# Issuing what follows a score group behind the group's last maximum on VectorE, in a decoder layer on one core

## The chip, the cores and the metric

The kernel runs on one core of one Trainium2 chip. The metric is the device time of one execution in microseconds (us). Three executions of the kernel before took 313.03, 313.59 and 314.9 us; their median, 313.59 us, is the time before. A further execution was profiled; it took 314.14 us.

## What is computed

One decoder layer on 256 tokens of width 1024, all in float32. Both head groups take q, k and v from one projection, their outputs are mixed by one output projection, a gated feed-forward layer follows, and each half ends in a layer norm:

```python
def reference(x, w_in, diff_lambda, diff_subln_g, w_o, ln1_g, ln1_b, w_ffn_in, w_ffn_out, ln2_g, ln2_b):
    ...
        proj = jnp.einsum('bsd,de->bse', x, w_in[l])
        dq, dk, dv, mq, mk, mv = jnp.split(proj, splits, axis=-1)
        a_out = diff_attention(dq, dk, dv, diff_lambda[l], diff_subln_g[l], lambda_init, cos, sin)
        b_out = moba_attention(mq, mk, mv, cos, sin)
        mix = jnp.einsum('bse,ed->bsd', jnp.concatenate([a_out, b_out], axis=-1), w_o[l])
        x = layer_norm(ALPHA * x + mix, ln1_g[l], ln1_b[l])
        gu = jnp.einsum('bsd,df->bsf', x, w_ffn_in[l])
        g, u = jnp.split(gu, 2, axis=-1)
        f = jnp.einsum('bsf,fd->bsd', jax.nn.silu(g) * u, w_ffn_out[l])
        x = layer_norm(ALPHA * x + f, ln2_g[l], ln2_b[l])
```

Differential attention takes the softmax of pairs of heads and subtracts one, times a factor, from the other. With 256 tokens the block-sparse attention is plain causal attention over one block. So both head groups compute eight causal softmaxes over scores of 256 queries by 256 keys.

## The kernel before

Every float32 product is split in two parts, `hi` (rounded) and `lo` (the rest), and summed from three matmuls (`mm3`, lines 150 to 153). Weights arrive in units of 1 MB (`raw`, four buffers); ScalarE casts a quarter of a unit at a time to `hi` (line 106) and VectorE subtracts to get `lo` (line 107). A buffer of `raw` comes free, and its next load is issued by SyncE, when the split of the unit before in it is done.

The input projection runs as `proj_qkT(0)` to `proj_qkT(3)` (q and k of the first group, then of the second) and `proj_v(4)`, `proj_v(5)`. Call c uses the units 2c and 2c+1. Each is a loop of 32 (or 16) steps n of three matmuls each, and other work is hung onto the steps of it by dictionaries, `side` (attention and rope) and `bg` (splits of the units to come), run at line 410. Scores of the first group are taken in two halves, `scores(0, 0)` and `scores(0, 1)`, at the steps 15 and 28 of `proj_qkT(2)`; those of the second group at the steps 5 and 11 of `proj_v(4)`.

One call of `scores(g, b)` (line 280) takes four PSUM buffers of the pool `psB`, which has four in all, fills them by 48 short matmuls (line 290), and then for each of the four sub-heads takes, on VectorE, the masked row maximum of a 128x128 and of a 128x256 piece (line 295; eight in all, each with a short read of its accumulator, and listed as CUSTOM_DVE in the trace and as ISA in the listing of the order), and on ScalarE the exponential of each (line 298). A buffer is free again when VectorE has taken both maxima of it. So the next group of scores needs the maxima of the group before.

`rope(c, bs, ps)` (line 244) has three VectorE operations that read the projection's PSUM (a shuffle into `sh`, line 253, and two products into `a` and `sh`, lines 254 and 255) and a `finish` (lines 258 to 260: an addition into `a`, a cast on ScalarE to `h`, and the subtraction to `l`). `plain` (line 264) is a cast and a subtraction (lines 269 and 270). `diff_combine` (line 312) runs at step 12 of `proj_qkT(3)`: a reciprocal `rl`, two small operations into `sc` (lines 315 to 317) and eight combinations on VectorE (line 320), two per head. From step 22 on `diff_pt(h)` transposes head h of the result on TensorE (lines 303 to 305).

Each engine runs its instructions in one order, fixed when the program is built. This order is not the order in which the code is written: a scheduler places every instruction on its engine at the time at which it expects it to be ready. `tc.issue_after(ins)` adds edges to it: what the block issues on the engine of `ins` is ordered behind `ins`, with no semaphore.

Of the kernel before, what the change touches and what calls it, by code (L numbers as in the profile page):

```python
# [37 lines left out]
FIN0, FIN1, FIN2, FIN3 = (20, 26), (4, 7), 31, 20  # L38
# [18 lines left out]
def hybrid_layer_kernel(ctx, tc, xT, xr, w_in, w_o, w_f1, w_f2, cols, rows, lamb, rot, tri, out):  # L57
    nc = tc.nc
# [65 lines left out]
    def spread(units_, pieces, steps):  # L124

        gens = [(u, p) for u in units_ for p in range(pieces)]
        live = {}

        def emit(u):
            if u not in live:  # L130
                live[u] = split_gen(u, pieces)
                state["split"] = u + 1
            next(live[u])

        hooks = {}
        for i, (u, p) in enumerate(gens):
            hooks.setdefault(i * steps // len(gens), []).append(lambda u=u: emit(u))
        return hooks

    def ahead(u, loads=4, splits=2):  # L140
        while state["load"] <= min(u + loads, NU - 1):
            n = state["load"]
            load_unit(n, LOAD_PIECES.get(n, 1))
            state["load"] += 1
        while state["split"] <= min(u + splits, NU - 1):
            n = state["split"]
            split_unit(n, SPLIT_PIECES.get(n, 2))
            state["split"] += 1

    def mm3(ps, sh, sl, mh, ml, first, last):  # L150
        nc.tensor.matmul(ps, sh, mh, start=first, stop=False)  # L151
        nc.tensor.matmul(ps, sh, ml, start=False, stop=False)  # L152
        nc.tensor.matmul(ps, sl, mh, start=False, stop=last)  # L153
# [81 lines left out]
    def qk_tiles(c, part):  # L235
        QH[c, part] = apool.tile([P, 2, S], F32R, tag=f"h{c % 2}{part}", name=f"h{c}_{part}")
        QL[c, part] = apool.tile([P, 2, S], F32R, tag=f"l{c % 2}{part}", name=f"l{c}_{part}")
# [7 lines left out]
    def rope(c, bs, ps):  # L245

        m = bs.stop - bs.start
        if bs.start == 0:
            qk_tiles(c, 0)
            SH[c] = rpool.tile([P, 2, S], F32, tag="sh", name=f"sh{c}", bufs=2)  # L250
            QA[c] = rpool.tile([P, 2, S], F32, tag="qk", name=f"a{c}", bufs=2)
        sh, a, h, l = SH[c][:, bs, :], QA[c][:, bs, :], QH[c, 0][:, bs, :], QL[c, 0][:, bs, :]
        nc.vector.stream_shuffle(sh, ps, SWAP)
        nc.vector.tensor_mul(a, ps, cos2[:, :m, :])
        nc.vector.tensor_mul(sh, sh, sin2[:, :m, :])

        def finish():
            nc.vector.tensor_add(a, a, sh)
            nc.scalar.copy(h, a)
            nc.vector.tensor_sub(l, a, h.bitcast(F32))  # L260

        return finish

    def plain(c, bs, ps):

        if bs.start == 0:
            qk_tiles(c, 1)
        h, l = QH[c, 1][:, bs, :], QL[c, 1][:, bs, :]
        nc.scalar.copy(h, ps)
        nc.vector.tensor_sub(l, ps, h.bitcast(F32))  # L270

    E0, E1, negm, ls, rl = {}, {}, {}, {}, {}

    def alloc_group(g):
        E0[g] = epool.tile([P, 8, P], F32, tag=f"E0", name=f"E0{g}", bufs=1)
        E1[g] = epool.tile([P, 8, S], F32, tag=f"E1", name=f"E1{g}", bufs=1)
        negm[g] = small.tile([P, 2, 8], F32, tag="negm", name=f"negm{g}")
        ls[g] = small.tile([P, 2, 8], F32, tag="ls", name=f"ls{g}")
        rl[g] = small.tile([P, 2, 8], F32, tag="rl", name=f"rl{g}")

    def scores(g, b):

        cq, ck = 2 * g, 2 * g + 1
        pr = [psB.tile([P, 3 * P], F32, tag="b", name=f"s{g}_{b}_{s}") for s in range(4)]
        terms = [(A, B, part) for A, B in ((QH, QH), (QL, QH), (QH, QL)) for part in range(2)]
        for q, o, n in ((slice(P, S), 0, S), (slice(0, P), S, P)):
            for m, (A, B, part) in enumerate(terms):
                for s in range(4):
                    r = slice(32 * s, 32 * s + 32)
                    nc.tensor.matmul(pr[s][:, o : o + n], A[cq, part][r, b, q], B[ck, part][r, b, :n],  # L290
                                     start=m == 0, stop=m == len(terms) - 1)
        for s in range(4):
            u = 4 * b + s
            for i, (e, p, m) in enumerate(((E0[g][:, u, :], pr[s][:, S:], mask[:, P:]), (E1[g][:, u, :], pr[s][:, :S], mask))):
                nc.vector.tensor_tensor_reduce(  # L295
                    out=e, in0=p, in1=m, scale=-0.125, scalar=3.4e38, op0=ALU.add, op1=ALU.min,
                    accum_out=negm[g][:, i, u : u + 1])
                nc.scalar.activation(e, e, AF.Exp, bias=negm[g][:, i, u : u + 1], scale=-1.0,  # L298
                                     accum_out=ls[g][:, i, u : u + 1])

# [92 lines left out]
    def proj_tok(ps, c, t, k):  # L393
        u, i = 2 * c + k // 4, k % 4
        ts_ = slice(t * P, (t + 1) * P)
        mm3(ps, xTh[:, k, ts_], xTl[:, k, ts_], hi[u][:, i, :], lo[u][:, i, :], k == 0, k == KT - 1)

    def proj_qkT(c, side):

        pool, tag = (psB, "b") if c == 1 else (psA, "acc")  # L400
        pss = [pool.tile([P, 2, S], F32, tag=tag, name=f"pj{c}_{b}") for b in range(4 if c < 2 else 2)]
        kb = {0: 1, 1: 4}.get(c, KT)
        order = [(j, k0 + k) for k0 in range(0, KT, kb) for j in range(4) for k in range(kb)]
        fin = []
        ahead(2 * c, splits=-1)
        bg = spread([1] + [2] if c == 0 else [3, 4, 5] if c == 1 else [2 * c + 2, 2 * c + 3], 4, 28)
        for n, (j, k) in enumerate(order):
            if n == 16:
                ahead(2 * c + 1, splits=-1)
            for f in side.get(n, []) + bg.get(n, []):  # L410
                f()
            u, i = 2 * c + k // 4, k % 4
            ws = slice(j * P, (j + 1) * P)
            ps = pss[j][:, 0, :] if c < 2 else pss[j // 2][:, j % 2, :]
            mm3(ps, hi[u][:, i, ws], lo[u][:, i, ws], xTh[:, k, :], xTl[:, k, :], k == 0, k == KT - 1)
            if k == KT - 1 and c < 2:
                done = [j] if c else list(range(4)) if j == 3 else []
                for jj in done:
                    bs, p1 = slice(jj % 2, jj % 2 + 1), pss[jj][:, 0:1, :]
                    if jj < 2:  # L420
                        fin.append(rope(c, bs, p1))
                    else:
                        plain(c, bs, p1)
            elif k == KT - 1 and j == 1:
                side.setdefault((FIN2, FIN3)[c - 2], []).append(rope(c, slice(0, 2), pss[0]))
            elif k == KT - 1 and j == 3:
                plain(c, slice(0, 2), pss[1])
        return fin

    def proj_v(c, side):  # L430

        pss = [psA.tile([P, 512], F32, tag="acc", name=f"pj{c}_{t}") for t in range(2)]
        ahead(2 * c, splits=-1)
        bg = spread([2 * c + 2, 2 * c + 3], 4, 14)
        for n, (t, k) in enumerate((t, k) for t in range(2) for k in range(KT)):
            if n == 8:
                ahead(2 * c + 1, splits=-1)
            for f in side.get(n, []) + bg.get(n, []):
                f()
            proj_tok(pss[t], c, t, k)  # L440
            if k == KT - 1:
                nc.scalar.copy(V[c - 4][:, t, :], pss[t])

    fin = proj_qkT(0, {})
    nlam, gsub = lambda_prep()
    fin = proj_qkT(1, {FIN0[i]: [f] for i, f in enumerate(fin)})
    nc.sync.dma_start(x_sb, xr.rearrange("(t p) d -> p t d", p=P))
    alloc_group(0)
    sc = {FIN1[i]: [f] for i, f in enumerate(fin)}
    for b in range(2):  # L450
        sc.setdefault(SCORES0[b], []).append(lambda b=b: scores(0, b))
    proj_qkT(2, sc)
    sc = {COMBINE: [diff_combine]}
    for h in range(4):
        sc.setdefault(DIFF_PT[h], []).append(lambda h=h: diff_pt(h))
    proj_qkT(3, sc)
    alloc_group(1)
    proj_v(4, {SCORES1[b]: [lambda b=b: scores(1, b)] for b in range(2)})
    od = {}

# [8 lines left out]
    for n, u in enumerate(range(6)):  # L469
        sd.setdefault(8 + n, []).append(lambda u=u: moba_pt(u))  # L470
    proj_v(5, sd)


# [376 lines left out]
```

## Time and profile before

| what | before |
|---|---|
| median of three executions | 313.59 us (313.03 to 314.9) |
| the profiled execution | 314.14 us |
| its span, first to last instruction | 312.4 us |
| TensorE busy | 300.0 us, 96% of the span |
| VectorE busy | 242.4 us, 78% |
| ScalarE busy | 178.8 us, 57% |
| TensorE's share of the chain that ended last | 88% |

Times within a profile count from the start of its span. An instruction's duration in a row holds some tail that overlaps with the next row, so what one costs in a row of its kind is read from the start of one to the start of the next. TensorE's matmuls are pipelined in the same way. The granted clock is told as a share of full speed: 1.00 is 2.4 GHz and 0.50 is 1.2 GHz.

### The profile page before, as it was taken

The page shows a single profiled execution, that of the slowest core. Times are in us where ns is not written, and L with a number is a line of the kernel's source. Part 1 is how long each engine was busy: PE and PEld are TensorE (multiplying, and loading weights), DVE is VectorE, ACT ScalarE, POOL GpSimd, SP SyncE. Part 2 cuts the span into 40 slices and gives each one's busy share as a digit, 9 for nine tenths or more (in the row PEclk, how much of TensorE's full clock was granted, in tenths as well). Part 3 has the DMA queues.
Part 4 walks back from the last instruction along what each step waited for, and adds up shares of the span by engine and source line. Part 5 has one row for each costly group of instructions (what it writes and reads, how often), then busy time and mean ns, then how long its engine had stood idle before and what let it go on. Part 6 is the DMA issues. An engine that isn't in the chain of part 4 may idle for free.

```text
span 312.4 us, 4858 instructions
## 1 busy us (share of the span) xinstructions
PE 300.0 (96%) x1838; PEld 257.6 (82%) x1838; DVE 242.4 (78%) x453; ACT 178.8 (57%) x346; POOL 9.0 (3%) x18
## 2 busy tenths in 40 slices
PE   7899979999999999999999999999999999999990
PEld 4799969988887788888888888888888888887880
DVE  3798987994677189939587897597778799897885
ACT  4765749477997228337367477457647665546000
POOL 1000000000030010200000000000000000000011
PEclk9999986999999999999999999999999999999997
DMA  6988993064048540576834744753560307652011
GB/s 196 366 265 305 421 371 141 2 229 177 0 141 292 210 169 19 209 311 218 322 102 169 268 148 141 253 185 144 211 234 38 134 19 273 243 155 120 0 67 67
DMA packets 13814, 57.25 MB, mean 183 GB/s; under 512 B 1696, under 2 KB 2464, under 8 KB 8928
## 3 DMA queue, kind: packets, MB, share of 16 engines
q1 hardware_dynamic: 13504, 54.86, 49.9%
q0 software_dynamic: 288, 2.10, 1.7%
q8 instruction: 14, 0.23, 0.3%
q14 instruction: 8, 0.07, 0.1%
HBM read 55.90 MB, written 1.05 MB: 182 GB/s over the span
## 4 chain that ended last, share of the span: by engine, by line
PE 88%; DVE 5%; DMA 2%; SPq 1%; issue 1%; ACT 0%; DVEq 0%
PE fc L612 21%; PE foc L694 13%; PE fc L613 11%; PE pj L151 6%; PE pj L153 6%; PE pj L152 6%; PE fo L694 4%; PE wo L151 3%; DMA raw<-in_w_in_dram 2%; PE fr L152 2%; PE fr L151 2%; PE wo L152 2%; PE wo L153 2%; PE fr L153 2%; PE s L290 2%; DVE lo L107 2%
## 5 line engine op out<-in xcount | busy, mean ns | idle before, releaser
L107 DVE TENSOR_TENSOR lo<-raw,hi 128x512 fp32r<-128x512 f32 (+2 forms) x116 | 105.9, 943 | 24.0 <-ACT hi L106 23.6
L106 ACT CAST hi<-raw 128x512 fp32r<-128x512 f32 (+2 forms) x116 | 90.5, 828 | 20.1 <-PE wo L153 9.9
L612 PE MATMUL fc<-x1T,hi 128*128 128x512 f32 x288 | 100.1, 392 | 0.0
L613 PE MATMUL fc<-x1T,lo 128*128 128x256 f32 x288 | 80.5, 280 | 0.0
L612 PEld LDWEIGHTS fc<-x1T,hi 128*128 128x128 f32 x288 | 54.0, 188 | 11.9
L613 PEld LDWEIGHTS fc<-x1T,lo 128*128 128x128 f32 x288 | 54.1, 188 | 0.0
L151 PE MATMUL pj<-xTh,hi 128*128 128x256 f32 x128 | 36.8, 294 | 1.7 <-ACT hi L201 1.0
L152 PE MATMUL pj<-xTl,hi 128*128 128x256 f32 x128 | 36.6, 289 | 0.1
L153 PE MATMUL pj<-xTh,lo 128*128 128x256 f32 x128 | 36.1, 291 | 0.0
L151 PEld LDWEIGHTS pj<-xTh,hi 128*128 128x128 f32 x128 | 24.8, 195 | 3.1 <-ACT hi L201 2.5
L615 ACT COPY v<-fc 128x256 f32<-128x256 f32 x36 | 13.3, 370 | 23.7 <-PE fc L613 23.6
L152 PEld LDWEIGHTS pj<-xTl,hi 128*128 128x128 f32 x128 | 25.0, 195 | 0.3 <-DVE xTl L188 0.3
L153 PEld LDWEIGHTS pj<-xTh,lo 128*128 128x128 f32 x128 | 24.5, 195 | 0.2
L616 DVE TENSOR_TENSOR v<-v,fc 128x256 f32<-128x256 f32 x36 | 15.0, 417 | 9.7 <-ACT v L615 9.6
L694 PE MATMUL foc<-hi,hTl 128*128 128x512 f32 x52 | 20.5, 395 | 0.0
L694 PE MATMUL foc<-lo,hTh 128*128 128x512 f32 x52 | 20.5, 395 | 0.0
L694 PE MATMUL foc<-hi,hTh 128*128 128x512 f32 x52 | 20.5, 394 | 0.0
L298 ACT ACTIVATE E<-E,negm 128x128 f32<-128x128 f32 (+1 forms) x32 | 14.1, 443 | 9.1 <-DVE negm L295 9.1
L151 PE MATMUL pj<-hi,xTh 128*128 128x512 f32 x32 | 13.5, 422 | 0.0
L619 ACT ACTIVATE v<-v 128x256 f32<-128x256 f32 x18 | 7.5, 419 | 9.9 <-DVE v L616 9.9
L151 PE MATMUL wo<-hi,mixh 128*128 128x512 f32 x32 | 12.9, 404 | 0.0
L151 PE MATMUL fr<-hi,x1T 128*128 128x512 f32 x32 | 12.9, 402 | 0.0
(187 smaller groups left out, 504.4 us busy)
## 6 DMA issues: line engine op xcount, KB each, us to landing
raw<-in_w_f_dram SPq DMA_DIRECT2D x28, 1024.0 KB, 5.1
raw<-in_w_in_dram SPq DMA_DIRECT2D x24, 256.0 KB, 5.8
raw<-in_w_in_dram SPq DMA_DIRECT2D x4, 1024.0 KB, 7.9
raw<-in_w_o_dram SPq DMA_DIRECT2D x4, 1024.0 KB, 5.0
raw<-in_w_f_dram SPq DMA_DIRECT2D x10, 256.0 KB, 4.0
raw<-in_w_f_dram SPq DMA_DIRECT2D x5, 512.0 KB, 5.3
raw<-in_w_in_dram SPq DMA_DIRECT2D x4, 512.0 KB, 8.1
rows<-in_rows_dram POOLq DMA_DIRECT2D x2, 1024.0 KB, 6.4
```

What stands on the lines that cost most here:

```text
L106: nc.scalar.copy(h, src)
L107: nc.vector.tensor_sub(l, src, h.bitcast(F32))
L151: nc.tensor.matmul(ps, sh, mh, start=first, stop=False)
L152: nc.tensor.matmul(ps, sh, ml, start=False, stop=False)
L153: nc.tensor.matmul(ps, sl, mh, start=False, stop=last)
L298: nc.scalar.activation(e, e, AF.Exp, bias=negm[g][:, i, u : u + 1], scale=-1.0, accum_out=ls[g][:, i, u : u + 1])
L612: nc.tensor.matmul(ps, hi[u][:, i, ws], x1T[:, k], start=k == 0, stop=False)
L613: nc.tensor.matmul(ps[:, 0, :], lo[u][:, i, ws], x1T[:, k, 0, :], start=False, stop=k == KT - 1)
L615: nc.scalar.copy(v, ps[:, 1, :])
L616: nc.vector.tensor_add(v, v, ps[:, 0, :])
L619: nc.scalar.activation(gate, gate, AF.Silu)
L694: nc.tensor.matmul(bank[name] if ps is None else ps, x, w[:, cs], start=key not in opened, stop=last and (m, i) == (len(todo) - 1, 2))
```

## The change

A variable `behind` remembers the last maximum that `scores` has issued. Whatever is run afterwards through the new `run` (the hooks of `side` and `bg` at the steps, and the `rope` and `plain` of the third and fourth projection) is ordered behind that maximum on VectorE. Before the first group there is nothing to be behind. No instruction is added or removed, and no operand or size changes. The orders of TensorE, GpSimd and SyncE stay as they were; those of VectorE and ScalarE change.

```diff
@@ -271,6 +271,13 @@
+    behind = {}
+
+    def run(*fs):
+        with tc.issue_after(behind["ins"]) if behind else ExitStack():
+            for f in fs:
+                f()
+
@@ -292,9 +299,9 @@
-                nc.vector.tensor_tensor_reduce(
+                behind["ins"] = nc.vector.tensor_tensor_reduce(
                     out=e, in0=p, in1=m, scale=-0.125, scalar=3.4e38, op0=ALU.add, op1=ALU.min,
-                    accum_out=negm[g][:, i, u : u + 1])
+                    accum_out=negm[g][:, i, u : u + 1]).ins
@@ -408,7 +415,7 @@
             for f in side.get(n, []) + bg.get(n, []):
-                f()
+                run(f)
@@ -422,9 +429,9 @@
-                side.setdefault((FIN2, FIN3)[c - 2], []).append(rope(c, slice(0, 2), pss[0]))
+                run(lambda: side.setdefault((FIN2, FIN3)[c - 2], []).append(rope(c, slice(0, 2), pss[0])))
             elif k == KT - 1 and j == 3:
-                plain(c, slice(0, 2), pss[1])
+                run(lambda: plain(c, slice(0, 2), pss[1]))
@@ -436,7 +443,7 @@
             for f in side.get(n, []) + bg.get(n, []):
-                f()
+                run(f)
```

The first place is VectorE around the first half of the first group's scores (`s0_0`; `lo7` and `hi7` are the split of weight unit 7, `pj2` is the third projection's PSUM, `sh2` and `a2` are its rope). Before:

```order
L107 TENSOR_TENSOR lo7_562<-raw7_408,hi7_561 128x512
L253 STREAM_SHUFFLE sh2_641<-pj2_0_499 128x512
L254 TENSOR_TENSOR a2_642<-pj2_0_499,cs_sb_132 128x512
L255 TENSOR_TENSOR sh2_641<-sh2_641,cs_sb_132 128x512
L107 TENSOR_TENSOR lo7_562<-raw7_408,hi7_561 128x512 x3
L258 TENSOR_TENSOR a2_642<-a2_642,sh2_641 128x512
L295 ISA E00_494,negm0_496<-s0_0_0_568,mask_133 128x128
```

And with the change:

```order
L107 TENSOR_TENSOR lo7_562<-raw7_408,hi7_561 128x512
L302 ISA E00_494,negm0_496<-s0_0_0_568,mask_133 128x128
...
L302 ISA E10_495,negm0_496<-s0_0_3_571,mask_133 128x256
L302 ISA negm0_496 128x1
L253 STREAM_SHUFFLE sh2_641<-pj2_0_499 128x512
L254 TENSOR_TENSOR a2_642<-pj2_0_499,cs_sb_132 128x512
L255 TENSOR_TENSOR sh2_641<-sh2_641,cs_sb_132 128x512
L107 TENSOR_TENSOR lo7_562<-raw7_408,hi7_561 128x512 x3
L302 ISA E00_494,negm0_496<-s0_1_0_690,mask_133 128x128
```

The eight maxima of `s0_0` now stand ahead of the seven operations that stood ahead of them, and six of these (all but the addition into `a2`) are now between the two halves' maxima.

The second place is VectorE from the last maximum of the second half (`s0_1`) to the first combination of `diff_combine` (`E00` and `E10`; `lo8` and `lo9` are splits of the units 8 and 9). Before, with the four `lo8` already ahead of the maxima of `s0_1`:

```order
L295 ISA E10_495,negm0_496<-s0_1_3_693,mask_133 128x256
L295 ISA negm0_496 128x1
L260 TENSOR_TENSOR l2_0_640<-a2_642,h2_0_639 128x512
L315 RECIPROCAL rl0_498<-ls0_497 128x16
L316 TENSOR_TENSOR sc_827<-ls0_497,rl0_498 128x8
L317 TENSOR_SCALAR sc_827<-sc_827,nlam_327 128x8
L270 TENSOR_TENSOR l2_1_774<-pj2_1_500,h2_1_773 128x512
L320 SCALAR_TENSOR_TENSOR E00_494<-E00_494,sc_827 128x128
```

And with the change:

```order
L258 TENSOR_TENSOR a2_642<-a2_642,sh2_641 128x512
L107 TENSOR_TENSOR lo8_782<-raw8_501,hi8_781 128x512 x3
L260 TENSOR_TENSOR l2_0_640<-a2_642,h2_0_639 128x512
L270 TENSOR_TENSOR l2_1_774<-pj2_1_500,h2_1_773 128x512
L107 TENSOR_TENSOR lo8_782<-raw8_501,hi8_781 128x512
L322 RECIPROCAL rl0_498<-ls0_497 128x16
L107 TENSOR_TENSOR lo9_846<-raw9_646,hi9_845 128x512
L323 TENSOR_TENSOR sc_827<-ls0_497,rl0_498 128x8
L107 TENSOR_TENSOR lo9_846<-raw9_646,hi9_845 128x512
L324 TENSOR_SCALAR sc_827<-sc_827,nlam_327 128x8
L253 STREAM_SHUFFLE sh3_857<-pj3_0_777 128x512
L327 SCALAR_TENSOR_TENSOR E00_494<-E00_494,sc_827 128x128
```

The addition into `a2`, the four `lo8`, two of the `lo9` and the shuffle of the fourth projection (`sh3`) now stand between the maxima of `s0_1` and the combinations. On ScalarE the cast `h2_0` has moved from ahead of the exponentials of `s0_1` to behind them, and `h3_0` from behind the first copy of a transposed head to behind the third.

## Rows read from the trace of the kernel before

**Rows 1.** The page: busy time and share of each engine, then the granted clock.

```profile
PE 300.0 (96%) x1838; PEld 257.6 (82%) x1838; DVE 242.4 (78%) x453; ACT 178.8 (57%) x346; POOL 9.0 (3%) x18
...
PEclk9999986999999999999999999999999999999997
```

**Rows 2.** Timeline, TensorE, 37 to 60 us: start us, us, engine line op.

```profile
37.58 0.28 PE L152 MATMUL pj<-xTl,hi 128*128 128x256 f32 x1
...
39.01 0.39 PE L290 MATMUL s<-l,h 32*128 32x128 f32 x8
39.32 0.38 PE L153 MATMUL pj<-xTh,lo 128*128 128x256 f32 x1
...
41.92 0.28 PE L153 MATMUL pj<-xTh,lo 128*128 128x256 f32 x1
43.97 0.84 PE L290 MATMUL s<-h,h 32*128 32x256 f32 x2 [1.77 <-DVE negm L295]
44.99 1.35 PE L290 MATMUL s<-h,h 32*128 32x256 f32 x6 [0.18 <-DVE negm L295]
...
48.29 0.58 PE L151 MATMUL pj<-xTh,hi 128*128 128x256 f32 x1
...
51.87 0.30 PE L152 MATMUL pj<-xTl,hi 128*128 128x256 f32 x1
...
59.34 0.27 PE L303 MATMUL ppd<-ident,E 128*128 128x128 f32 x1
```

**Rows 3.** Windows: stretch, its us, each engine's busy us, PEclk, DMA share, GB/s.

```profile
8.00:10.00 2.00, 0.97 (x8) 0.76 (x6) 1.15 (x3) 1.24 (x2) 0.00 (x0) 1.00 0.98 345
42.00:45.50 3.50, 1.44 (x5) 0.59 (x3) 3.49 (x19) 1.99 (x9) 0.00 (x0) 0.94 0.91 323
46.00:51.00 5.00, 5.00 (x57) 4.88 (x54) 3.33 (x11) 4.30 (x14) 0.00 (x0) 0.50 0.18 72
```

**Rows 4.** Timeline, VectorE, 38 to 59 us.

```profile
38.97 0.73 DVE L253 STREAM_SHUFFLE sh<-pj 128x512 f32<-128x512 f32 x1
...
42.59 0.68 DVE L258 TENSOR_TENSOR a<-a,sh 128x512 f32<-128x512 f32 x1
43.19 0.28 DVE L295 CUSTOM_DVE_ANT_0 E<-s,mask 128x128 f32<-128x128 f32 x1
...
47.67 2.50 DVE L107 TENSOR_TENSOR lo<-raw,hi 128x512 fp32r<-128x512 f32 x4 [2.18 <-ACT hi L106]
50.09 0.29 DVE L295 CUSTOM_DVE_ANT_0 E<-s,mask 128x128 f32<-128x128 f32 x1
...
52.30 0.69 DVE L260 TENSOR_TENSOR l<-a,h 128x512 fp32r<-128x512 f32 x1
54.07 0.25 DVE L315 RECIPROCAL rl<-ls 128x16 f32<-128x16 f32 x1 [1.07 <-ACT E L298]
...
54.69 0.68 DVE L270 TENSOR_TENSOR l<-pj,h 128x512 fp32r<-128x512 f32 x1
55.29 2.71 DVE L320 SCALAR_TENSOR_TENSOR E<-E,sc 128x128 f32<-128x128 f32 x8
57.93 0.68 DVE L107 TENSOR_TENSOR lo<-raw,hi 128x512 fp32r<-128x512 f32 x1
...
58.54 0.73 DVE L253 STREAM_SHUFFLE sh<-pj 128x512 f32<-128x512 f32 x1
```

**Rows 5.** Timeline, ScalarE, 43 to 50 us.

```profile
43.52 0.40 ACT L298 ACTIVATE E<-E,negm 128x128 f32<-128x128 f32 x1 [4.95 <-DVE negm L295]
...
47.03 2.17 ACT L106 CAST hi<-raw 128x512 fp32r<-128x512 f32 x4
49.10 0.62 ACT L259 CAST h<-a 128x512 fp32r<-128x512 f32 x1
```

**Rows 6.** DMA, issues in 28.3 to 29.5 (unit 8), then in 33 to 36 (unit 9): us to landing.

```profile
raw<-in_w_in_dram SPq DMA_DIRECT2D x1, 1024.0 KB, 11.8
...
raw<-in_w_in_dram SPq DMA_DIRECT2D x1, 1024.0 KB, 9.0
```

## The prediction

> **What bounds the kernel now.** I read the page first: TensorE is busy 96% of the span and its granted clock falls in one place only, the seventh of forty slices [rows 1]. So the time is TensorE's, and something goes wrong once, near 47 us. I then followed TensorE's timeline through that place. The first half of the first score group is inserted cheaply: from the last projection matmul before it (37.58) to the first one behind it (39.32) pass 1.74 us. The second half takes from 41.92 to 48.29, 6.37 us for the same 48 matmuls, and TensorE is named as waiting for VectorE's maxima [rows 2]. Those are late: the first half was complete when its last row ended, at 39.01 + 0.39 = 39.4 [rows 2], yet VectorE began the first maximum at 43.19, since the shuffle, two products, three `lo7` and the addition stand ahead of it from 38.97 on [rows 4]. Until then the four PSUM buffers are full and the second half can't be written. The wait has a second price. In 42.0 to 45.5 TensorE is busy 1.44 of 3.50 us, and then in 46 to 51 the granted clock is 0.50, which is 1.2 GHz [rows 3]; the matmuls from 48.29 to 51.87 go at that pace [rows 2].
>
> **What goes.** With the change the maxima stand right behind the first `lo7`, which ends about where the shuffle started, at 39.0. They wait for the scores, so they start at 39.42. Eight maxima take 52.30 - 50.09 = 2.21 us [rows 4], so the buffers are free at 41.63. TensorE wants the first of them about 0.2 after 41.92. It need not wait, and the clock has no reason to fall. Two terms:
> - the second half costs 1.74 instead of 6.37: **4.63 us** saved;
> - at half clock, 16 matmul steps take 51.87 - 48.29 = 3.58. At full clock the 21 steps from 39.32 to 41.92 take 2.60, 0.124 each, so 16 take 1.98: **1.60 us** saved.
>
> Together 6.23. TensorE would be at the first transpose of `diff_pt(0)` at 59.34 - 6.23 = 53.11 [rows 2].
>
> **What comes.** The operations that were ahead of the maxima now come behind them, and all of them before the combinations which that transpose needs. VectorE was at its first combination at 55.29, 4.05 us before TensorE came for it [rows 2, 4]; it had that slack only because TensorE was late. Its new chain, each piece from start to start in [rows 4]:
> - 39.42 + 2.21 (maxima, first half) = 41.63;
> - shuffle, products and three `lo7`, as from 38.97 to 42.59: 3.62, to 45.25. The second half of the scores is complete by about 43.7 (42.1 + 1.6), so nothing waits;
> - maxima, second half: 2.21, to 47.46;
> - addition into `a2`, 42.59 to 43.19: 0.60, to 48.06;
> - three `lo8`, at (50.09 - 47.67) / 4 = 0.605: 1.82, to 49.88;
> - `l2_0`, `l2_1` and the last `lo8`, at 0.60 (as from 54.69 to 55.29): 1.80, to 51.68;
> - reciprocal and the two `sc`, 54.07 to 54.69: 0.62, and two `lo9` between them: 1.21, to 53.51;
> - shuffle `sh3`: its row of 0.73 less about 0.1 of overlap, 0.62, to 54.13;
> - both combinations of head 0, (57.93 - 55.29) / 4 = 0.66, to 54.79;
> - VectorE to TensorE: the first score matmul of the second half began 0.78 after the first maximum (43.97 against 43.19), of which two maxima are 0.55, so 0.2: **55.0**.
>
> TensorE arrives at 53.11 and waits **1.89 us**, a wait that the kernel before doesn't have. Heads 1 to 3 follow at 0.66 each while TensorE takes three projection steps, over 1 us, between them, so they are ready.
>
> ScalarE must not be later than this chain. Its exponentials start 0.33 behind the first maximum (43.52 against 43.19) and take 3.51 per half [rows 5]: 39.75 to 43.26. The `hi8` casts, 2.07, end at 45.33; unit 8 landed at 28.5 + 11.8 = 40.3 [rows 6]. The second half's exponentials run from 45.58 to 49.09, the cast `h2_0` to 49.71 [rows 5], against 49.88 when VectorE wants it. That cover is thin, 0.2 us; each tenth beyond it would be a tenth of waiting. The reciprocal wants the exponentials at 51.68 and has 2.6 us in hand. The cast and subtraction of `h2_1` have 0.4 to spare by a cast of the same length.
>
> All other edits cost nothing. The second group's maxima also change places with `lo10` and `lo11`, but there VectorE already stood idle and TensorE did not wait for it; the clock's digits are full from there to the tail [rows 1]. The loads that take the buffers of units 7 and 8 are issued later with those splits, by 2.6 us (the last `lo7` ends at 45.25 instead of 42.6) and 1.6 us (51.68 instead of 50.1). They are for units 11 and 12, which belong to the last projection and the output projection; a whole projection's matmuls lie before their use, and a load has taken 9 to 12 us at its worst here [rows 6], so they stay hidden.
>
> **Sum.** 6.23 - 1.89 = 4.34 us, or in one step 59.34 - 55.0. The bounds of the new wait are nothing (all 6.23 is kept) and the wait that it resembles, with its clock (6.23 given back, nothing gained). I take 1.89, since nearly every piece of the chain has a row. Behind the transposes the orders are those of before, relative to TensorE, which is busy without a gap, so 4.34 us reaches the end. The profiled execution took 314.14, 0.55 above the median of the three timed. 314.14 - 4.34 = 309.8, and on the scale of the median **309.3 us**.
>
> **Rivals.**
> (A) *The clock falls at the new wait.* For: it fell after the wait at 42. Against: that wait lasted, with a few matmuls in it, from 42.0 to 45.5, nearly twice as long; and in 8 to 10 us TensorE stood still for 1.03 of 2.00 us and the granted clock stayed at 1.00 [rows 3]. The new wait lies between the two. If it fell for as long as before, from 45.5 to 51.8, the loss is 6.3 x (1 - 1.98 / 3.58) = 2.8 us: gain 1.5, median 312.1. The Trainium skill, TensorE: Matmul & The Clock Gate, section "HAM oscillation — how this bites in real kernels", tells of a kernel that waits for data between bursts of matmuls and has its clock put back each time; by that rule, taken strictly, the change would move the half-clock stretch by some ten microseconds instead of removing it, and the sum would be 1.5. The 46 to 51 row agrees with it, the 8 to 10 row shows a wait that was too short, and no row here shows one of 1.9.
> (B) *No new wait*: if the combinations came early enough after all, all 6.23 would be kept, median 307.4. Against: it needs 1.9 us out of a chain that has rows throughout.
> (C) *Slower, by unit 9.* Two `lo9` now stand ahead of the combinations, and they need unit 9's load and `hi9`. In the kernel before, that unit's split came after the combinations. It was issued before 36 and took 9.0, so it was there by 45 [rows 6], and `hi9` starts at 50. If its `lo9` came 3.1 us later than about 52, the wait at the transposes would be 5.0, and the clock would fall as before: 5.0 + 2.8 - 6.23 = 1.6 lost, median 315.2. The point from which it decides is a wait of 6.23 - 2.8 = 3.4, or 1.5 us of delay over my 1.89. Against: the load has some 5 us in hand.
> (D) *No effect*: the wait at 42 has another cause, such as the weights of the next step. Against: the trace names the maxima, and the first score matmul follows them by a constant step. Median 313.6.
>
> **How the numbers follow.** Forecast 0.79, A 0.11, B 0.04, C 0.03, D 0.03. What a measurement can tell from no change is about 0.5%, 1.6 us. Forecast and B are faster; A is faster in perhaps a third of its cases (a shorter time at half clock), otherwise the same; D is the same. So faster 0.86, same 0.11, slower 0.03. The three runs of before spread from -0.6 to +1.3 around their median, so the forecast alone is 308.7 to 310.6. With A at its full price on one side, and on the other a wait half as long (308.4) with part of that spread, the range is 308.0 to 312.1.
>
> **What would show it.** In the new profile: the first maximum at about 39.4; the second half of the scores entered without a wait at 42.1 and left at about 43.7; no stretch at 0.50 near 48; VectorE without `l2_0` waiting long for ScalarE; TensorE waiting about 1.9 us at 53 for line 327, the combinations; the last projection reached 4.3 us earlier. I am wrong if the transposes wait for something else or not at all, if a granted clock of 0.50 stands at about 55 to 61 us, or if a later stage opens a gap that takes the 4.3 us back.

## The result, and the profile after

The changed kernel took **310.27 us** (median of 4 runs, 309.22 to 310.65) against 313.67 for the kernel before in the same comparison (4 runs, 313.03 to 314.9): a ratio of 0.9882 with a 95% interval of 0.9842 to 0.9922. A second comparison, of 6 and 11 runs, gave 309.44 against 314.08: 0.9865 (0.983 to 0.99). The change is faster by 1.2 to 1.4%; the forecast of 309.3 us was a ratio of 0.9863.

The page of the changed kernel: busy time by engine, and the granted clock in 40 slices.

```profile
PE 296.7 (96%) x1838; PEld 254.9 (83%) x1838; DVE 241.4 (78%) x453; ACT 178.7 (58%) x346; POOL 9.0 (3%) x18
...
PEclk9999999999999999999999999999999999999998
```

Against [rows 1] TensorE has the same number of instructions and 3.3 us less busy time, and the slices of its clock with an 8 and a 6 are gone: only the last one, the tail, is under 9.

The timeline of TensorE in the changed kernel, 37 to 78 us, answers to [rows 2]; columns as there.

```profile
38.16 0.51 PE L297 MATMUL s<-h,h 32*128 32x256 f32 x8
...
39.69 0.39 PE L153 MATMUL pj<-xTh,lo 128*128 128x256 f32 x1
...
42.29 0.28 PE L153 MATMUL pj<-xTh,lo 128*128 128x256 f32 x1
42.50 0.52 PE L297 MATMUL s<-h,h 32*128 32x256 f32 x8
...
44.04 0.39 PE L151 MATMUL pj<-xTh,hi 128*128 128x256 f32 x1
...
53.28 0.28 PE L153 MATMUL pj<-xTh,lo 128*128 128x256 f32 x1
54.72 0.30 PE L310 MATMUL ppd<-ident,E 128*128 128x128 f32 x1 [1.15 <-DVE E L327]
55.02 0.33 PE L311 MATMUL ppd<-ident,E 128*128 128x128 f32 x1
...
55.22 0.36 PE L151 MATMUL pj<-xTh,hi 128*128 128x256 f32 x1
...
77.26 1.05 PE L337 MATMUL dpv<-V,ptd 128*128 128x128 f32 x8
```

The second score half goes from 42.29 to 44.04, 1.75 us, with no wait named; before it was 6.37. What is new is the wait of 1.15 us ahead of the first transpose, for the combinations of line 327. The row counts idle time from the end of the matmul before, 53.28 + 0.28. Counted from when the transpose would have begun without it, 0.12 after 53.28 as the other steps do, it is 54.72 - 53.40 = 1.32.

The second transpose is held up once more. The first one needs only the first combination of head 0, the second needs the second combination. The timeline of TensorE's weight loads (PEld; each matmul has one ahead of it) in the changed kernel, 53 to 56 us, names that wait:

```profile
55.02 0.14 PEld L311 LDWEIGHTS ppd<-ident,E 128*128 128x128 f32 x1 [0.19 <-DVE E L327]
```

So the three transposes take 0.50 us to the next projection matmul (54.72 to 55.22), where the three of the kernel before, without a wait, take 0.24 (59.34 to 59.58). In all TensorE loses 1.32 + 0.26 = 1.58 us here.

The windows of the changed kernel, for TensorE alone (stretch, its us, busy us, granted clock, DMA share, GB/s), answer to [rows 3]:

```profile
45.00:53.00 8.00, 8.00 (x70) 1.00 0.39 133
53.00:55.00 2.00, 0.85 (x6) 1.00 0.78 246
55.00:60.00 5.00, 5.00 (x43) 1.00 0.28 115
```

The stretch at 0.50 is gone, and none stands behind the new wait.

The timeline of VectorE in the changed kernel, 39 to 55 us, answers to [rows 4]:

```profile
39.80 0.29 DVE L302 CUSTOM_DVE_ANT_0 E<-s,mask 128x128 f32<-128x128 f32 x1 [0.39 <-PE s L297]
...
42.03 0.74 DVE L253 STREAM_SHUFFLE sh<-pj 128x512 f32<-128x512 f32 x1
...
45.65 0.29 DVE L302 CUSTOM_DVE_ANT_0 E<-s,mask 128x128 f32<-128x128 f32 x1
...
47.88 0.69 DVE L258 TENSOR_TENSOR a<-a,sh 128x512 f32<-128x512 f32 x1
...
50.29 0.69 DVE L260 TENSOR_TENSOR l<-a,h 128x512 fp32r<-128x512 f32 x1
...
52.09 0.25 DVE L322 RECIPROCAL rl<-ls 128x16 f32<-128x16 f32 x1
...
53.61 0.73 DVE L253 STREAM_SHUFFLE sh<-pj 128x512 f32<-128x512 f32 x1
54.23 2.05 DVE L327 SCALAR_TENSOR_TENSOR E<-E,sc 128x128 f32<-128x128 f32 x6
```

From the first maximum on, nothing on VectorE waits, down to the combinations at 54.23.

Executions differ in how long the start of the kernel takes, so the stages are compared from the first matmul of the first score group on. That matmul is at 38.16 above and here at 37.79 in the kernel before, whose timeline of TensorE has these two rows:

```profile
37.79 0.51 PE L290 MATMUL s<-h,h 32*128 32x256 f32 x8
...
81.62 0.60 PE L330 MATMUL dpv<-V,ptd 128*128 128x128 f32 x4
```

The times from there on for every kernel of this study, by the names that stand beside the experiments below (us from that first matmul to the first matmul of each later stage in the same timeline, one profiled execution each):

| kernel | 2nd half | first transpose | 2nd group's scores | its 2nd half | `dpv` |
|---|---|---|---|---|---|
| before | 6.18 | 21.55 | 29.99 | 35.91 | 43.83 |
| after | 4.34 | 16.56 | 25.25 | 31.17 | 39.10 |
| r_after | 4.34 | 16.55 | 25.25 | 31.18 | 39.10 |
| e1_first_half | 4.35 | 16.20 | 24.91 | 32.07 | 39.99 |
| e2_second_group | 6.27 | 21.42 | 29.87 | 35.79 | 43.71 |
| e3_late_pt | 4.34 | 17.37 | 23.67 | 29.59 | 37.52 |
| e4_wait | 4.33 | 17.36 | 25.37 | 31.29 | 39.22 |
| e5_wait_long | 4.34 | 18.97 | 25.49 | 31.41 | 39.33 |
| e7_scalar_order | 4.33 | 16.21 | 24.91 | 31.47 | 39.90 |
| e8_wait_pinned | 4.34 | 18.96 | 29.22 | 35.15 | 43.07 |
| e9_before_late | 6.26 | 23.31 | 29.60 | 35.54 | 43.46 |
| e10_cast_last | 4.34 | 16.21 | 24.90 | 31.06 | 39.50 |
| e11_cast_early | 4.34 | 16.54 | 25.23 | 31.15 | 39.08 |

Two executions of the changed kernel agree within 0.01 us at every stage. With the old wait and its half-clock stretch the profiles agree less well: `before` and `e2_second_group` differ by 0.12 us at `dpv`, and `e9_before_late`, whose edit moves only the transposes, is 0.37 us ahead of `before`. So a tenth can be read here between kernels without that stretch, and some 0.4 us against kernels with it. By `dpv` the change has gained 43.83 - 39.10 = 4.73 us, or 4.4 to 4.7 with those other two in the place of `before`.

### The profile page after: what moved, and what is told of

It reads as the page before. It is cut to its first block, busy times and chain, and to the rows that moved or that the text cites. A ratio compares the mean times of both kernels' runs of the same rounds, so it can differ in the third digit from the quotient of the medians.

```text
span 308.2 us, 4858 instructions
## 1 busy us (share of the span) xinstructions
PE 296.7 (96%) x1838; PEld 254.9 (83%) x1838; DVE 241.4 (78%) x453; ACT 178.7 (58%) x346; POOL 9.0 (3%) x18
## 4 chain that ended last, share of the span: by engine, by line
PE 90%; DVE 6%; DMA 2%; SPq 1%; issue 1%; ACT 0%; DVEq 0%
PE fc L619 21%; PE foc L701 13%; PE fc L620 11%; PE pj L151 6%; PE pj L153 6%; PE pj L152 6%; PE fo L701 5%; PE wo L151 3%; PE fr L152 2%; PE fr L151 2%; PE wo L152 2%; PE wo L153 2%; PE fr L153 2%; DMA raw<-in_w_in_dram 2%; DVE lo L107 2%; PE s L297 2%
## 5 line engine op out<-in xcount | busy, mean ns | idle before, releaser
L152 PE MATMUL pj<-xTl,hi 128*128 128x256 f32 x128 | 35.9, 284 | 0.0
```

## The experiments

The theory was the prediction's: the whole gain is the first group's second half and the clock behind it, and what is given back is one wait at the first transpose. The rivals asked whether other edges of the change matter, whether that wait costs more than its length, and what it takes for the clock to fall there.

**The changed kernel once more** (r_after), to see the spread.

> The changed kernel once more. Its four runs were 309.22, 309.95, 310.59 and 310.65 us, the first two with a mean granted clock of 0.997, the last two with 0.988 and 0.987. My theory (the gain is the wait of the second score half and the half-clock stretch behind it, less a new wait of 1.3 to 1.6 us at the first transpose): the new wait lets the clock fall in some executions and not in others, so two kinds of runs appear again, some 1 to 3 us apart, the longer ones with the lower clock. Rival: the clock differs in the tail or at the start, where it costs nothing, and time and clock don't go together.

Measured: 309.44 (308.57 to 310.88, 6 runs). The profiled execution of it took 310.88, the longest, and shows where such an execution loses its time. The window from 10 to 15 us of TensorE in this execution:

```profile
10.00:15.00 5.00, 4.73 (x26) 0.66 1.04 390
```

In the first profile of the change that stretch had a clock of 1.00. Here the score group starts at 39.31 instead of 38.16, and from there to `dpv` the two agree to 0.01 us. So what made this execution longer than the first lies ahead of the changed place, and not at the new wait: the theory was wrong. The rival was right that the clock differs at the start, and wrong that it costs nothing there.

**Only the first half's maxima hold back what follows.** (e1_first_half)

```
-                behind["ins"] = nc.vector.tensor_tensor_reduce(...).ins
+                mx = nc.vector.tensor_tensor_reduce(...).ins
+                if (g, b) == (0, 0):
+                    behind["ins"] = mx
```

> Only what follows the first score half is ordered behind its maxima; all later maxima stay where the scheduler puts them, so four lo8 stand ahead of the second half's maxima and no lo9 and no shuffle ahead of the combinations. My theory: the wait of the second score half and the half clock are gone as with the whole change (6.2 us), and the combinations come at about 53.9 instead of 54.2, so the new wait is 0.8 us or so and the time is that of the whole change or up to 1 us less: 309 to 310.3. Rival (the gain needs the whole new order, the second half's maxima ahead of lo8 and the second group's too): it keeps half of the gain or less, 312 or more.

Measured: 310.25 (309.68 to 310.37, 6 runs), ratio 0.9887 (0.9855 to 0.9918). The second half has no wait, so this edge alone makes the saving. But `dpv` comes 0.89 us later than in the whole change, although the first transpose comes 0.36 earlier. The loss is at the second group's scores; timelines of TensorE, then of ScalarE, in this kernel:

```profile
53.92 0.30 PE L312 MATMUL ppd<-ident,E 128*128 128x128 f32 x1 [0.78 <-DVE E L329]
...
62.63 0.39 PE L297 MATMUL s<-h,h 32*128 32x256 f32 x3
63.24 0.88 PE L297 MATMUL s<-h,h 32*128 32x256 f32 x5 [0.23 <-ACT ptd L316]
...
65.40 0.50 PE L151 MATMUL pj<-hi,xTh 128*128 128x512 f32 x1
```

```profile
54.70 0.48 ACT L316 COPY ptd<-ppd 128x384 f32<-128x384 f32 x1
59.87 0.62 ACT L259 CAST h<-a 128x512 fp32r<-128x512 f32 x1 [4.70 <-DVE a L258]
60.40 0.47 ACT L316 COPY ptd<-ppd 128x384 f32<-128x384 f32 x1
...
62.70 0.49 ACT L316 COPY ptd<-ppd 128x384 f32<-128x384 f32 x1
63.07 0.60 ACT L269 CAST h<-pj 128x512 fp32r<-128x512 f32 x1
```

The cast `h3_0` stands ahead of the copy `ptd1` and waits 4.70 us for VectorE's addition; the three copies behind it, and with them the PSUM buffers, are late. The last copy ends at 63.19, and the score matmuls that need its buffer begin at 63.24. Behind that copy stands the cast of `plain`, `h3_1` (line 269), to 63.67, and behind the cast its subtraction on VectorE, to 64.40; the scores need both, and these two are named as waited for as well (0.3 and 0.2 us). In all the score block takes 62.63 to 65.40, 2.77 us, where the change has 1.53. The whole change has `h3_0` behind `ptd2`. That was the new suspicion: an order on ScalarE that I had priced at nothing.

**Only the second group's maxima.** (e2_second_group) The same edit with `g == 1` for the condition.

> The edges of the second score group alone: its maxima change places with lo10 and lo11 as in the whole change, everything around the first group is as before. My theory: nothing, TensorE doesn't wait there, 313.0 to 314.5, with the wait of 42 us and the half clock as before. Rival (the second group has a share in the gain): 0.8 us faster or more.

Measured: 313.79 against 313.76, ratio 0.9989 (0.9965 to 1.0014). No effect, as expected; the old wait stands in the timeline of TensorE as before:

```profile
43.98 2.37 PE L297 MATMUL s<-h,h 32*128 32x256 f32 x8 [1.87 <-DVE negm L302]
```

**The change with later transposes** (e3_late_pt), so that TensorE comes for them after the combinations.

```
-COMBINE, DIFF_PT = 12, (22, 25, 28, 31)
+COMBINE, DIFF_PT = 12, (28, 29, 30, 31)
```

> The whole change, and the four transposes of the combined scores moved from steps 22, 25, 28, 31 of the fourth projection to 28, 29, 30, 31. TensorE then reaches the first of them at about 55.5, behind the combination at about 54.9. My theory: the new wait of 1.3 to 1.6 us goes, and with it the clock's fall where there is one: 308.0 to 308.8, all runs with a clock near 0.997. Rival (the wait only moves, to the scores of the second group, which need ScalarE behind these transposes): no change, 309.5 to 310.6.

Measured: **307.52** (307.27 to 309.55, 6 runs), ratio 0.9813 (0.9777 to 0.9849); this beats both kernels, and is 0.5 below my range. The transposes wait for nothing, and TensorE has no idle time from 53 to 60; windows, then timeline:

```profile
53.00:58.00 5.00, 5.00 (x45) 1.00 0.62 213
58.00:60.00 2.00, 2.00 (x17) 1.00 0.00 0
```

```profile
56.70 0.28 PE L153 MATMUL pj<-xTh,lo 128*128 128x256 f32 x1
56.82 0.27 PE L310 MATMUL ppd<-ident,E 128*128 128x128 f32 x1
```

`dpv` comes 1.58 us earlier than in the change: the wait of 1.32, and 0.26 for that of the second transpose.

**The same edit on the kernel before** (e9_before_late), as the counterpart.

> The kernel before, with only the transposes moved to the steps 28 to 31. My theory: nothing, 313.0 to 314.5, since TensorE didn't wait for the combinations there; the 1.9 us of the same move under the whole change are the new wait and nothing else. Rival (late transposes are better by themselves): 1 us faster or more.

Measured: 313.93 (10 runs), ratio 1.0002 (0.9979 to 1.0025). Later transposes alone bring nothing that the medians show. The 0.37 us at `dpv` stood there ahead of the first transpose: the six steps take 17.37 - 15.24 = 2.13 us by the kernels without the old wait, which puts `before` at 23.68, and this run has 23.31. So the gain of the run above is the new wait's.

**Longer waits, first try.** (e4_wait) VectorE gets four unused copies (128x256) ahead of the combinations.

```
+        idle = epool.tile([P, S], F32, name="idle")
+        for _ in range(4):
+            last = nc.vector.tensor_copy(idle, E1[0][:, 1, :])
+        wait = tc.issue_after(last.ins)
+        wait.__enter__()
...
```

> The whole change, and four copies of 128x256 on VectorE that nothing reads, ordered ahead of the combinations; the new wait of TensorE at the first transpose grows by about 1.3 us, to about 2.9. My theory without a fall of the clock: 1.3 us more than the whole change, 311.0 to 311.9. If the longer wait lets the clock fall, as after the wait of the kernel before: up to 2.8 us more on top, 313 to 314.5, with a granted clock of 0.50 for some 6 us behind it.

**And the second try** (e5_wait_long), four subtractions (128x512) in their place.

> The whole change, and four subtractions of 128x512 on VectorE that nothing reads, about 0.6 us each, ordered ahead of the combinations, so that TensorE stands still at the first transpose for about 3.6 us instead of 1.15. If the clock then falls, as behind the wait of the kernel before: 2.45 us for the wait and up to 2.8 for the clock, 313 to 315, and a stretch at 0.50 in the profile. If it doesn't fall behind a wait of this length: 311.5 to 312.5, granted clock 1.00 throughout that stage.

Measured: 309.22 (308.92 to 309.41, 6 runs) and 309.47 (308.71 to 311.44, 4 runs). Both missed: the wait did not grow as meant. The first transpose in the timelines of TensorE of the two kernels:

```profile
55.05 0.30 PE L310 MATMUL ppd<-ident,E 128*128 128x128 f32 x1 [1.49 <-DVE E L332]
```

```profile
56.65 0.30 PE L310 MATMUL ppd<-ident,E 128*128 128x128 f32 x1 [1.55 <-DVE E L332]
```

The copies cost 0.2 us each, less than I had assumed. In both kernels projection matmuls had also come ahead of the transposes: in the second, the last one ahead of them starts 17.15 us after the scores where the change has 15.12. The scheduler had filled most of the wait with other work. The profiles show only that here 1.49 and 1.55 us left the clock at 1.00.

**The wait pinned** (e8_wait_pinned): the four subtractions, and the projection's matmuls from that step on kept behind the transposes.

```
...
+        turned[name] = nc.tensor.transpose(ps[:, 2, :], e1[:, P:], ident).ins
...
+            with tc.issue_after(turned["d0"]) if "d0" in turned else ExitStack():
                 mm3(ps, hi[u][:, i, ws], lo[u][:, i, ws], xTh[:, k, :], xTl[:, k, :], k == 0, k == KT - 1)
...
```

> The whole change with four subtractions of 128x512 (an unused result) on VectorE ahead of the combinations, and the projection's matmuls from the step of the first transposes on kept behind those transposes, so that TensorE can't put other matmuls into the wait. The combinations start some 2.4 to 3 us later, so the wait at the first transposes is about 3.9 to 4.5 us where the change has 1.15. Theory (TensorE's clock stays full over it): the time is that of the change plus the growth of the wait less what the scores of the second group no longer wait, 311.5 to 312.5 us, and the granted clock is 1.00 in the 5 us after the wait. Rival A of the prediction (a long enough wait takes the clock to half): granted clock about 0.5 in a stretch after the wait, and 1.5 us more, 313 to 314 us.

Measured: 313.45 (312.49 to 314.59, 10 runs), ratio 0.9995 (0.9974 to 1.0015). The timeline of TensorE in this kernel, then the window behind the wait:

```profile
52.42 0.28 PE L153 MATMUL pj<-xTh,lo 128*128 128x256 f32 x1
56.26 0.30 PE L310 MATMUL ppd<-ident,E 128*128 128x128 f32 x1 [3.56 <-DVE E L332]
...
57.31 0.28 PE L152 MATMUL pj<-xTl,hi 128*128 128x256 f32 x1
...
57.57 0.41 PE L151 MATMUL pj<-xTh,hi 128*128 128x256 f32 x1
...
60.55 0.41 PE L153 MATMUL pj<-xTh,lo 128*128 128x256 f32 x1
...
60.95 0.27 PE L311 MATMUL ppd<-ident,E 128*128 128x128 f32 x1
```

```profile
58.00:60.00 2.00, 2.00 (x11) 0.50 0.00 0
```

The wait is 3.56 us long, and the clock falls to its lower level, 1.2 GHz, shortly after it: matmuls of 0.28 become 0.41 at about 57.5, and from 60.8 on they are fast again. From the first transpose to `dpv` pass 43.07 - 18.96 = 24.11 us where the change has 22.54. So a wait longer by 2.40 costs 2.40 and another 1.57 by the clock, and the gain is gone (0.76 us of it are left at `dpv`, nothing that the medians show). So the theory was wrong and rival A is real as a mechanism; the change's wait of 1.15 did not set it off in either of its two profiles.

**ScalarE's order, first try** (e7_scalar_order): only the first half's edge, with `FIN3`, the step at which the second group's addition and cast are written, moved from 20 to 29.

> The first score half alone ordered behind its maxima, as in the first experiment, and the rope of the fourth projection finished at step 29 instead of 20, so that on ScalarE the cast h3_0 stands behind the first three copies of transposed heads instead of behind the first alone. My theory: in that experiment h3_0 waited 4.7 us for VectorE's addition and held up the copies, whose PSUM buffers the second group's scores need; with the cast moved this wait of 0.9 to 1.2 us goes, 308.9 to 309.5, level with the whole change or a little under it. Rival (the copies were late for another reason): no change from that experiment, 310.2.

Measured: 310.97 (309.94 to 312.08, 6 runs), ratio 0.9898 (0.9867 to 0.9929). The forecast missed, and the run does not separate theory and rival: the addition moved on VectorE too, and the cast now waits ahead of `ptd3`, in the timeline of ScalarE:

```profile
60.63 0.62 ACT L259 CAST h<-a 128x512 fp32r<-128x512 f32 x1 [2.98 <-DVE a L258]
```

**The cast alone** (e10_cast_last): the first half's edge, the addition left at its step, the cast behind the copy of `ptd2`.

```
...
+                def cast(f):
+                    with tc.issue_after(copied['d2']):
+                        f((1,))
...
+                        side.setdefault(FIN3, []).append(lambda: f((0,)))
+                        side.setdefault(31, []).append(lambda: cast(f))
...
```

> Edges only behind the first half's maxima (as in e1), and in addition ScalarE's cast of the second group's rotated queries, h3_0, stands behind the copy of ptd2, as it does in the whole change; VectorE and TensorE keep e1's order. Theory (the part of the gain that e1 lacks, 0.8 us, is ScalarE's order: the cast waits for VectorE's addition in front of the copies of ptd1 and ptd2, and the transposed buffers come free late): 309.4 us (309.0 to 309.8), the matmuls of the second group's first score half back to back, its block 1.6 to 1.8 us where e1 has 2.8. Rival (what e1 lacks is on VectorE or TensorE, or nothing at all): 310.2 us as e1, the gap ahead of the second group's scores stays.

Measured: 309.82 (309.37 to 310.48, 6 runs), ratio 0.9875 (0.9852 to 0.9898): between the two. The second group's first half is nearly free of waits (24.90 to 31.06 with the projection steps, 6.16, where the first edge alone has 7.16), which is 1.0 us for one cast's place. But half of it is lost again in the second half. Timelines of TensorE and VectorE in this kernel:

```profile
69.11 1.01 PE L299 MATMUL s<-h,h 32*128 32x256 f32 x8
...
71.15 0.50 PE L151 MATMUL pj<-hi,xTh 128*128 128x512 f32 x1
```

```profile
63.66 3.69 DVE L107 TENSOR_TENSOR lo<-raw,hi 128x512 fp32r<-128x512 f32 x6
67.27 0.28 DVE L304 CUSTOM_DVE_ANT_0 E<-s,mask 128x128 f32<-128x128 f32 x1
```

Six `lo` stand ahead of the second group's first maximum, which begins at 67.27, 29.22 us after the first score matmul (38.05); the whole change has it at 65.04, 26.88 after its own. From the addition into the second group's `a` to that maximum VectorE has ten `lo` here and with the first edge alone, and four in the whole change. With the buffers free late, the second half takes 71.15 - 69.11 = 2.04 us until the projection goes on, where the first edge alone has 1.54. So part of the theory holds, and another part of what the first edge alone lacks is on VectorE. Whether it needs the edge behind the first group's second half, those of the second group or both isn't tested.

**The change with the cast early** (e11_cast_early): the edge is on ScalarE alone, where the copy of `ptd1` now stands behind the cast. On VectorE only two `lo` change places with the subtractions beside them.

```
-            nc.scalar.copy(h, a)
+            cast[c] = nc.scalar.copy(h, a).ins
...
-        nc.scalar.copy(pt, ps)
+        with tc.issue_after(cast[3]) if name == 'd1' else ExitStack():
+            nc.scalar.copy(pt, ps)
```

> The whole change, but ScalarE's copy of ptd1 stands behind the cast h3_0; VectorE and TensorE keep the order of the change. Theory (ScalarE's order is worth 0.8 to 0.9 us): 310.3 us (309.9 to 310.8) where the whole change has 309.4; the cast waits 3 to 5 us for VectorE's addition, and TensorE waits ahead of the second group's scores. Rival (the order on ScalarE costs nothing, as the prediction had it): 309.4 us, no such wait on TensorE.

Measured: 309.39 (308.73 to 310.26, 6 runs), ratio 0.9863 (0.9838 to 0.9887): the rival. The timeline of ScalarE in this kernel says why:

```profile
58.03 1.66 ACT L106 CAST hi<-raw 128x512 fp32r<-128x512 f32 x3 [1.91 <-PE pj L152]
59.60 0.62 ACT L259 CAST h<-a 128x512 fp32r<-128x512 f32 x1
60.13 1.22 ACT L315 COPY ptd<-ppd 128x384 f32<-128x384 f32 x3
```

The three `hi10` casts went ahead of the cast `h3_0` here, so the three copies follow it at once and the last ends at 61.35, 2.2 us before the scores at 63.56. With the first edge alone the same casts stood between the copies, and the last copy ended at 63.19. VectorE's addition, which `h3_0` waits for, also begins earlier here: 58.81 - 38.33 = 20.48 us after the first score matmul, against 59.10 - 37.72 = 21.38. Which of the two would have been enough isn't tested. So the cast's place alone costs nothing here. What costs is that the last copy, and the cast and subtraction of `plain` behind it, end after TensorE has come for them.

## Why the prediction was right, point by point

- *What goes, 6.23 us*: right. The second half takes 1.75, as forecast (1.74), and the half-clock stretch is gone. TensorE's arrival at the first transpose is 21.55 - 15.24 = 6.31 us earlier, and so is `dpv` in the kernel without the new wait (43.83 - 37.52). Against the kernel before with the same late transposes it is 43.46 - 37.52 = 5.94, so the size is known to some 0.4. The edge that makes this is the first half's alone.
- *What comes, a wait of 1.89 us*: right in kind, place and cause, too long by 0.57, or by 0.31 with the 0.26 that the second transpose adds. TensorE's own arrival was right: 15.24 us after the scores (15.12 and one step), against 21.55 - 6.23 = 15.32. VectorE's chain from the first maximum to the transpose took 54.72 - 39.80 = 14.92, not 55.0 - 39.42 = 15.58. Two pieces were mis-sized. From the reciprocal to the shuffle `sh3` I counted 1.83, adding the small operations to two full `lo9`; it took 53.61 - 52.09 = 1.52. From the first combination to the transpose I counted 0.86, two combinations and a hand-over of 0.2; it took 54.72 - 54.23 = 0.49, since the first transpose needs one combination only. The second transpose, which needs two, began at 55.02, 0.79 behind. The other pieces were within 0.03.
- *The sum, 4.34 us*: the change had 21.55 - 16.56 = 4.99 at the transposes and 4.73 at `dpv`. The 0.26 between is the second transpose's wait. Against the sum the gain is larger by 0.39: 0.31 for the wait, 0.08 for TensorE's arrival. The medians show 313.67 - 310.27 = 3.40 and 314.08 - 309.44 = 4.64; the stage times are the sharper measure, and the clock in 10 to 15 us is one thing that moves single executions. That the second median lies 0.14 from the forecast of 309.3 and the first 0.97 is chance, since the kernel is the same.
- *ScalarE's cover of 0.2 us*: it held. The cast `h2_0` runs from 49.52 to 50.13, and its subtraction on VectorE at 50.29 without a wait.
- *"All other edits cost nothing"*: true of the whole change, but for a reason that I had not given. I looked for clocks and idle VectorE. The orders on ScalarE and VectorE between 54 and 68 us matter to about 1 us. With the first edge alone they come out worse by 1.25 us behind the transposes (0.89 at `dpv` and the lead of 0.36), and the whole change's further edges put that right. Moving one cast takes back 0.5 of it.
- *Rival A*: its price was 2.8 at a wait of 1.89. At 3.56 the clock did fall, at a price of 1.57; at 1.15 and at 1.55 it did not. Where between these it begins isn't known, and near 10 us a wait of 1.85 was followed by the lower clock in one execution and one of 1.95 was not in another (last section). So at the 1.89 that I forecast rival A might have come true, though no run shows a wait of that length at that place; that the wait came out shorter was luck. The section "HAM oscillation — how this bites in real kernels" of the Trainium skill, TensorE: Matmul & The Clock Gate, tells of a kernel whose waits between bursts of matmuls put its clock back each time. The run at 3.56 us agrees with it. The waits that it tells of are longer than 1.89 us, so the prediction read it too strictly, and the change, with 1.00 behind its wait of 1.15, does not speak against it.
- *Rivals B, C and D* are out: there is a wait; it is VectorE's combinations and not unit 9, whose `lo9` at 52.25 had no wait; and the old wait did come from the maxima.

## What to carry to other kernels

When a wait is taken away, time the new chain on the engine that held it up down to the next operation that anyone waits for: here a saving of 6.2 us shrank to 4.7 there, and moving the waiting step by six places got the rest. Then check that copies which free shared buffers end before the consumer comes, on every engine whose order the edges move: edges that seem to do nothing can be what keeps that order good.

## What the runs showed of the hardware

- A wait of nearly the same length left the clock full in one execution and not in another. In both profiles of the changed kernel TensorE waits near 10 us for the first split weights, 1.95 us in the first and 1.85 in the second:

```profile
10.23 0.39 PE L151 MATMUL pj<-xTh,hi 128*128 128x256 f32 x1 [1.95 <-ACT hi L201]
```

```profile
10.27 0.38 PE L151 MATMUL pj<-xTh,hi 128*128 128x256 f32 x1 [1.85 <-ACT hi L201]
```

  The granted clock in 10 to 15 us is 1.00 in the first and 0.66 in the second, and the second comes 1.15 us later to the score group. In the second, TensorE had also waited 0.27 us at 5.33. What decides it was not found.
- Behind the wait of 3.56 us the first 1.1 us of matmuls (56.26 to about 57.4) still ran at full speed; the half speed came after them, for some 3.2 us.
